# A two-layer hybrid trunk: scalings, first taps and key copies moved from VectorE to ScalarE, and the two components of differential attention combined in one step

## The chip, the cores and the metric

The kernel runs on one core of a Trainium2 chip. The metric is the time of one launch on the device, in microseconds (us), as the median of several executions. Engines are named as in the profile: PE is TensorE's matrix multiply and PEld its weight load, DVE is VectorE, ACT is ScalarE, POOL is GpSimd and SP is the queue that starts most of the DMA transfers. Each engine works its own queue strictly in order and waits on semaphores where an instruction needs another engine's result.

## The reference, cut to what matters

The program is a decoder trunk of two layers for 256 tokens of width 1024. In each layer a norm and one input projection `z = h @ w_in` (2964 columns) feed four head groups of 4 heads by 64, called A, B, C and D. Their outputs go through `w_out` into the residual, and a SwiGLU block of width 2816 follows. What the change touches:

- A (sparse attention): three softmax branches, two of which (selected blocks and window) have `o = g1 * softmax(s1) @ v1 + g2 * softmax(s2) @ v2` with gates per token and head.
- B (differential attention): `a = p[0] - lam * p[1]`, where `p` is the softmax of two score components over the same keys, then `o = rmsnorm(a @ v, sub_g) * (1 - lam_init)`. The norm divides by the root of `mean(o*o) + EPS` with EPS = 1e-6.
- C (mLSTM): a causal convolution with four taps and a bias over the 256 channels of `u`, then SiLU, then projections to q and k.
- D (dilated attention) and B both turn rotated q and k to channel-major form before their scores.

## The kernel before

All matrix products over the weights are done in three passes at full fp32 accuracy: a weight block is loaded to `wraw`, ACT rounds it to `whi` (line 224), DVE takes the rest `wlo = wraw - whi` (line 225), and `product` (lines 229 to 231) multiplies hi by hi, hi by lo and lo by hi. So each block of 128 by 1024 weights costs one ACT and one DVE instruction besides the PE work.

The input projection runs over six chunks of up to 512 columns. While PE works on the chunks, and then on `w_out`, the four mixers are laid between: each is a generator, and the table `ORDER` says how many steps of which generator are written out behind which chunk (Z and A are the two parts of A; lower-case letters transpose a finished output). That is the order of writing only. The framework's planner then sets the order on each engine from its own estimate of what is ready and how urgent it is, so in the trace the instructions of a mixer and of the projection stand finely mixed. Nothing changes order on the chip: what an engine's queue has first, it does first.

The places that the steps below name:

- A, lines 471 to 517: for each of two 128-token tiles `t` and two rounds `r`, scores come to PSUM, ACT takes the exponentials with their row sums (line 492), DVE inverts the sums and multiplies in the gates (lines 495, 496), and DVE scales the four probability matrices in place (line 499), 128 or 256 columns each. PE then transposes them (line 506, `pTa`), ACT and DVE split the result (lines 509, 510) and PE applies the values (line 516). There are eight such groups of four in the run: two layers, two tiles, two rounds.
- C, lines 579 to 599: `u` is transposed on PE, copied to `uT` on ACT (line 583), convolved on DVE (first tap with bias on line 587, three more on line 589, twice per layer), passed through tanh on ACT (593), finished on DVE (594), and projected on PE (599, `qkc`).
- `qk_T`, lines 669 to 683, for B and D: after POOL's rotation (`rope`) and PE's transposes, ACT copies q (681) and DVE copies k (682).
- B, lines 689 to 738: for each tile and each `i` two score components `c` for two heads `b`. Exponentials with row sums on ACT (707), inverses on DVE (709), times minus lambda (710), the second component scaled (712) and the combination (713), then transposes, values, and the norm, whose `rstd_of` adds EPS and takes the power -0.5 on POOL (239, 243) before POOL's final product (736).

Of the kernel before, what the change touches and what calls it, by code (L numbers as in the profile page):

```python
# [10 lines left out]
F32 = mybir.dt.float32  # L11
F32R = mybir.dt.float32r
BF = mybir.dt.bfloat16
AF = mybir.ActivationFunctionType
OP = mybir.AluOpType
# [3 lines left out]
P = 128  # L19
SEQ = 256  # L20
D = 1024
NH = 4
# [6 lines left out]
EPS = 1e-6  # L29
# [69 lines left out]
def trunk(ctx, tc, xt, w_in, w_out, w_gu, w_dn, gains, gfin, cmpw, chan, rowp, ident_d, kf, kb, out):  # L99
    nc = tc.nc  # L100
    V, S, G, T = nc.vector, nc.scalar, nc.gpsimd, nc.tensor
# [40 lines left out]
    def t4():  # L142
        i = 2 * D_IN + slot[0] % NS * 1024
        slot[0] += 1
        return cur['big'][:, i:i + 1024]
# [84 lines left out]
        T.matmul(acc, xh, wl, start=False, stop=False)  # L230
        T.matmul(acc, xl, wh, start=False, stop=last)  # L231

    def rstd_of(ms, shape, name):
        e = sm.tile([P] + shape, F32, name=name + "e")
        r = sm.tile([P] + shape, F32, name=name)
        n = 1
        for s in shape:
            n *= s
        G.tensor_scalar(e, ms, EPS, None, op0=OP.add)
        nh = nhalf[:, :n]  # L240
        if len(shape) == 2:
            nh = nh.rearrange("p (a b) -> p a b", a=shape[0])
        G.tensor_tensor(out=r, in0=e, in1=nh, op=OP.pow)
        return r
# [65 lines left out]
    def heads(ap, n):  # L310
        return ap.rearrange("p (n w) -> p n w", n=n)
# [145 lines left out]
    def mixer_a2(l, z, d):  # L457
# [13 lines left out]
        for t in range(2):  # L471
# [3 lines left out]
            for r in range(2):  # L475
# [20 lines left out]
                V.tensor_tensor(out=zs, in0=zs, in1=g4[:, t, r], op=OP.mult)  # L496
                for b in range(2):
                    for m in range(2):
                        V.tensor_scalar(pm[:, b, m, 0:ns * P], pm[:, b, m, 0:ns * P], zs[:, b, m:m + 1], None,  # L499
                                        op0=OP.mult)  # L500
                for s in range(ns):
                    pt = aux("pTa")
                    for b in range(2):
# [23 lines left out]
    def mixer_c(l, z, d, o):  # L527
# [56 lines left out]
        uc = q512("uc")  # L584
        cw = d['conv']
        for b in range(2):
            V.tensor_scalar(uc[:, b], uT[:, b, 3:259], cw[:, b, 3:4], cw[:, b, 4:5], op0=OP.mult, op1=OP.add)
            for j in (2, 1, 0):
                V.scalar_tensor_tensor(out=uc[:, b], in0=uT[:, b, j:j + 256], scalar=cw[:, b, j:j + 1], in1=uc[:, b],
                                       op0=OP.mult, op1=OP.add)  # L590
# [13 lines left out]
        qT, kT = qk  # L604
# [64 lines left out]
    def qk_T(z, col, n, hd, scale, tag, eng):  # L669
        pq = aux("qT" + tag)  # L670
        pk = aux("kT" + tag)
        for t in range(2):
            rr = w512("rqk")
            rope(eng, heads(z[:, t, col:col + 512], n), n, hd, t, heads(rr, n))
            for b in range(2):
                T.transpose(pq[:, b * SEQ + t * P:b * SEQ + (t + 1) * P], rr[:, b * P:(b + 1) * P], ident)
                T.transpose(pk[:, b * SEQ + t * P:b * SEQ + (t + 1) * P], rr[:, 256 + b * P:256 + (b + 1) * P], ident)
            yield
        qT = q512("qT" + tag)
        kT = q512("kT" + tag)  # L680
        S.activation(qT, heads(pq, 2), AF.Copy, scale=scale)
        V.tensor_copy(kT.rearrange("p b t -> p (b t)"), pk)
        return qT, kT


    def mixer_b(l, z, d, o):
        qT, kT = yield from qk_T(z, COL['bq'], 16, 16, 32.0 ** -0.5, "b", G)
        yield
        for t in range(2):
            n = P * (t + 1)  # L690
            am = heads(t4(), 4)
            for i in range(2):
                zb = sm.tile([P, 2, 2], F32, name="zb")
                nmb = sm.tile([P, 2, 2], F32, name="nmb")
                pmb = t4().rearrange("p (c b k) -> p c b k", c=2, b=2)

                scs = [heads(aux("sb")[:, 0:2 * n], 2) for _ in range(2)]
                for b in range(2):
                    for c, sc in enumerate(scs):
                        q = slice(32 * (2 * i + c), 32 * (2 * i + c) + 32)  # L700
                        T.matmul(sc[:, b], qT[q, b, t * P:(t + 1) * P], kT[q, b, 0:n], start=b == 0, stop=False)  # L701
                for sc in scs:
                    T.matmul(sc[:, :, t * P:(t + 1) * P], kbc('ident'), heads(kbc('causal'), 2), start=False, stop=True)
                for c, sc in enumerate(scs):
                    V.tensor_reduce(out=nmb[:, c], in_=sc, op=OP.max, axis=AX.X, negate=True)
                    for b in range(2):
                        S.activation(pmb[:, c, b, 0:n], sc[:, b], AF.Exp, bias=nmb[:, c, b:b + 1],
                                     accum_out=zb[:, c, b:b + 1])
                V.reciprocal(out=zb, in_=zb)
                V.tensor_scalar(zb[:, 1], zb[:, 1], d['nlam'], None, op0=OP.mult)  # L710
                for b in range(2):
                    V.tensor_scalar(pmb[:, 1, b, 0:n], pmb[:, 1, b, 0:n], zb[:, 1, b:b + 1], None, op0=OP.mult)
                    V.scalar_tensor_tensor(out=am[:, 2 * b + i, 0:n], in0=pmb[:, 0, b, 0:n], scalar=zb[:, 0, b:b + 1],
                                           in1=pmb[:, 1, b, 0:n], op0=OP.mult, op1=OP.add)
                yield
            aT = t4().rearrange("p (s h k) -> p s h k", s=2, h=NH)
            for s in range(t + 1):
# [14 lines left out]
            V.tensor_tensor(out=ob, in0=p4, in1=d['subg'][:, None, :].to_broadcast([P, NH, HD]), op=OP.mult)  # L732
            ms = sm.tile([P, NH], F32, name="bms")
            V.tensor_reduce(out=ms, in_=sq, op=OP.add, axis=AX.X)
            rr = rstd_of(ms, [NH], "brs")
            G.tensor_tensor(out=heads(o[:, t], 4), in0=ob, in1=rr[:, :, None].to_broadcast([P, NH, HD]),
                            op=OP.mult)
            yield
# [442 lines left out]
```

## Time and profile before

| | |
|---|---|
| median of 3 runs | 696.52 us (694.51 to 696.61) |
| the profiled execution's own time | 698.92 us |
| its span, first to last instruction | 697.1 us |
| PE busy | 673.1 us, 97% of the span |
| DVE busy | 473.8 us, 68% |
| ACT busy | 350.9 us, 50% |
| POOL busy | 111.3 us, 16% |
| mean granted clock of TensorE | 0.992 |

The busy share is an average over stages with different limits. A wait row names the engine that waited, the line and tile of the waiting instruction, and what ended the wait last, with the total time, the number of times and the longest. "issue" stands for time for which the profile shows no releaser. A timeline row gives start, duration, engine, line, operation, output and inputs, shape and count; several equal instructions in a row are merged, and the duration is then that of the whole run of them.

### The profile page before, as it was taken

How to read it: one execution, taken by the hardware profiler on the slowest of the kernel's cores; microseconds unless marked ns; L12 is line 12 of the kernel's file. 1: busy time of each engine (PE TensorE's matmuls, PEld its weight loads, DVE VectorE, ACT ScalarE, POOL GpSimd, SP SyncE). 2: the span in 40 equal slices, each digit the busy share in tenths (PEclk: the TensorE clock that was granted, in tenths of full speed). 3: DMA queues.
4: the chain of work that ended last, by engine and by line, in shares of the span. 5: the costliest groups of instructions: out<-in, count | busy, mean ns of one | idle time of the engine just before them, and what ended most of it. 6: DMA issues, size and time to landing. Idle time of an engine off the chain costs nothing.

```text
span 697.1 us, 11878 instructions
## 1 busy us (share of the span) xinstructions
PE 673.1 (97%) x4701; PEld 607.8 (87%) x4701; DVE 473.8 (68%) x730; ACT 350.9 (50%) x585; POOL 111.3 (16%) x118
## 2 busy tenths in 40 slices
PE   8989899999999999999999999999999999999996
PEld 5766677899999999999987667789999999998885
DVE  6698689758766766644577688995776575755443
ACT  7555556546444444433366455574635454444333
POOL 0151354100201110000012353621000000000002
PEclk9999999999999999999999899999999999999998
DMA  8863323235576656666656423322566556666641
GB/s 274 305 198 102 100 65 118 62 92 182 152 209 183 179 162 206 180 187 183 187 175 207 145 71 91 91 62 61 150 207 187 157 179 188 184 208 198 190 121 61
DMA packets 31879, 109.11 MB, mean 157 GB/s; under 512 B 3920, under 2 KB 4688, under 8 KB 31824
## 3 DMA queue, kind: packets, MB, share of 16 engines
q1 hardware_dynamic: 31392, 107.82, 51.5%
q8 instruction: 37, 0.61, 0.4%
q10 hardware_dynamic: 432, 0.54, 0.2%
q14 instruction: 18, 0.15, 0.1%
HBM read 107.30 MB, written 1.05 MB: 155 GB/s over the span
## 4 chain that ended last, share of the span: by engine, by line
PE 85%; DVE 9%; issue 2%; ACT 2%; DMA 1%; POOL 0%; SPq 0%; POOLq 0%; ACTq 0%; DVEq 0%
PE f L229 12%; PE f L230 12%; PE f L231 12%; PE dn L230 5%; PE dn L229 5%; PE dn L231 5%; PE zp L230 4%; PE zp L231 4%; PE zp L229 4%; DVE wlo L225 2%; PE op L230 2%; PE op L229 2%; PE op L231 2%; PE sb L701 1%; DVE zbig L499 1%
## 5 line engine op out<-in xcount | busy, mean ns | idle before, releaser
L225 DVE TENSOR_TENSOR wlo<-wraw,whi 128x1024 fp32r<-128x1024 f32 (+2 forms) x201 | 245.4, 1223 | 153.1 <-ACT whi L224 152.8
L224 ACT ACTIVATE whi<-wraw 128x1024 fp32r<-128x1024 f32 (+2 forms) x201 | 210.5, 1048 | 245.3 <-PE f L230 110.3
L229 PE MATMUL f<-hT,whi 128*128 128x256 f32 x704 | 199.8, 284 | 0.0
L230 PE MATMUL f<-lT,whi 128*128 128x256 f32 x704 | 199.3, 283 | 0.0
L231 PE MATMUL f<-hT,wlo 128*128 128x256 f32 x704 | 199.2, 283 | 0.0
L230 PEld LDWEIGHTS f<-lT,whi 128*128 128x128 f32 x704 | 135.0, 192 | 0.1
L229 PEld LDWEIGHTS f<-hT,whi 128*128 128x128 f32 x704 | 135.0, 192 | 0.1
L231 PEld LDWEIGHTS f<-hT,wlo 128*128 128x128 f32 x704 | 135.0, 192 | 0.0
L229 PE MATMUL zp<-whi,hT 128*128 128x512 f32 (+1 forms) x192 | 76.5, 401 | 1.0 <-ACT whi L224 1.0
L230 PE MATMUL zp<-wlo,hT 128*128 128x512 f32 (+1 forms) x192 | 76.3, 398 | 0.6 <-DVE wlo L225 0.5
L231 PE MATMUL zp<-whi,lT 128*128 128x512 f32 (+1 forms) x192 | 75.1, 392 | 0.0
L230 PE MATMUL dn<-gT,whi 128*128 128x256 f32 x176 | 49.5, 281 | 0.0
L229 PE MATMUL dn<-gT,whi 128*128 128x256 f32 x176 | 49.5, 281 | 0.0
L231 PE MATMUL dn<-gT,wlo 128*128 128x256 f32 x176 | 49.5, 281 | 0.0
L229 PEld LDWEIGHTS zp<-whi,hT 128*128 128x128 f32 x192 | 36.9, 192 | 7.4 <-ACT whi L224 1.8
L230 PEld LDWEIGHTS zp<-wlo,hT 128*128 128x128 f32 x192 | 36.7, 191 | 7.4 <-DVE wlo L225 2.2
L231 PEld LDWEIGHTS zp<-whi,lT 128*128 128x128 f32 x192 | 36.6, 191 | 5.7
L230 PE MATMUL op<-oT,whi 128*128 128x256 f32 x128 | 37.1, 290 | 0.0
L231 PE MATMUL op<-oT,wlo 128*128 128x256 f32 x128 | 36.7, 287 | 0.0
L229 PE MATMUL op<-oT,whi 128*128 128x256 f32 x128 | 36.5, 289 | 0.0
L230 PEld LDWEIGHTS dn<-gT,whi 128*128 128x128 f32 x176 | 33.1, 188 | 0.0
L229 PEld LDWEIGHTS dn<-gT,whi 128*128 128x128 f32 x176 | 33.1, 188 | 0.0
(283 smaller groups left out, 1067.8 us busy)
## 6 DMA issues: line engine op xcount, KB each, us to landing
wraw<-in_w_gu_dram SPq DMA_DIRECT2D x88, 512.0 KB, 4.2
wraw<-in_w_dn_dram SPq DMA_DIRECT2D x44, 512.0 KB, 4.1
wraw<-in_w_in_dram SPq DMA_DIRECT2D x39, 512.0 KB, 4.3
wraw<-in_w_out_dram SPq DMA_DIRECT2D x16, 512.0 KB, 3.7
wraw<-in_w_in_dram SPq DMA_DIRECT2D x8, 404.0 KB, 3.1
wraw<-in_cmpw_dram SPq DMA_DIRECT2D x4, 512.0 KB, 6.0
xr<-in_xt_dram SPq DMA_DIRECT2D x4, 256.0 KB, 6.2
chan<-in_chan_dram SPq DMA_DIRECT2D x2, 261.0 KB, 5.1
```

The lines of the kernel that those rows point to most:

```text
L224: S.activation(hi[:, c], raw[:, c], AF.Copy)
L225: V.tensor_tensor(out=lo[:, c], in0=raw[:, c], in1=hi[:, c].bitcast(F32), op=OP.subtract)
L229: T.matmul(acc, xh, wh, start=first, stop=False)
L230: T.matmul(acc, xh, wl, start=False, stop=False)
L231: T.matmul(acc, xl, wh, start=False, stop=last)
L499: V.tensor_scalar(pm[:, b, m, 0:ns * P], pm[:, b, m, 0:ns * P], zs[:, b, m:m + 1], None, op0=OP.mult)
L701: T.matmul(sc[:, b], qT[q, b, t * P:(t + 1) * P], kT[q, b, 0:n], start=b == 0, stop=False)
```

## The change

Four edits. In A, line 499's scaling becomes an ACT copy with a scale per token. In C, line 587's first tap becomes an ACT instruction with scale and bias per channel. In `qk_T`, the copy of k becomes an ACT copy like that of q. In B, the first component is no longer divided by its row sum z0: the second is multiplied by `nlam * z0 / z1` and added to the first as it stands, in one DVE instruction in place of two. The row of B's output is then too large by the factor z0, and since a norm follows, the same factor is taken out by it, if the norm's epsilon is multiplied by z0 squared: `zq = EPS * z0 * z0` is one small DVE instruction per tile, and `rstd_of` adds it as a tensor in place of the constant.

```diff
-    def rstd_of(ms, shape, name):
+    def rstd_of(ms, shape, name, eps=None):
...
-        G.tensor_scalar(e, ms, EPS, None, op0=OP.add)
+        if eps is None:
+            G.tensor_scalar(e, ms, EPS, None, op0=OP.add)
+        else:
+            G.tensor_tensor(out=e, in0=ms, in1=eps, op=OP.add)
...
-                        V.tensor_scalar(pm[:, b, m, 0:ns * P], pm[:, b, m, 0:ns * P], zs[:, b, m:m + 1], None,
-                                        op0=OP.mult)
+                        S.activation(pm[:, b, m, 0:ns * P], pm[:, b, m, 0:ns * P], AF.Copy, scale=zs[:, b, m:m + 1])
...
-            V.tensor_scalar(uc[:, b], uT[:, b, 3:259], cw[:, b, 3:4], cw[:, b, 4:5], op0=OP.mult, op1=OP.add)
+            S.activation(uc[:, b], uT[:, b, 3:259], AF.Identity, bias=cw[:, b, 4:5], scale=cw[:, b, 3:4])
...
-        V.tensor_copy(kT.rearrange("p b t -> p (b t)"), pk)
+        S.activation(kT, heads(pk, 2), AF.Copy)
...
+            z0 = sm.tile([P, 2, 2], F32, name="zb0")
             for i in range(2):
-                zb = sm.tile([P, 2, 2], F32, name="zb")
+                z1 = sm.tile([P, 2], F32, name="zb1")
...
                         S.activation(pmb[:, c, b, 0:n], sc[:, b], AF.Exp, bias=nmb[:, c, b:b + 1],
-                                     accum_out=zb[:, c, b:b + 1])
-                V.reciprocal(out=zb, in_=zb)
-                V.tensor_scalar(zb[:, 1], zb[:, 1], d['nlam'], None, op0=OP.mult)
+                                     accum_out=z1[:, b:b + 1] if c else z0[:, b, i:i + 1])
+                V.reciprocal(out=z1, in_=z1)
+                V.scalar_tensor_tensor(out=z1, in0=z1, scalar=d['nlam'], in1=z0[:, :, i], op0=OP.mult, op1=OP.mult)
                 for b in range(2):
-                    V.tensor_scalar(pmb[:, 1, b, 0:n], pmb[:, 1, b, 0:n], zb[:, 1, b:b + 1], None, op0=OP.mult)
-                    V.scalar_tensor_tensor(out=am[:, 2 * b + i, 0:n], in0=pmb[:, 0, b, 0:n], scalar=zb[:, 0, b:b + 1],
-                                           in1=pmb[:, 1, b, 0:n], op0=OP.mult, op1=OP.add)
+                    V.scalar_tensor_tensor(out=am[:, 2 * b + i, 0:n], in0=pmb[:, 1, b, 0:n], scalar=z1[:, b:b + 1],
+                                           in1=pmb[:, 0, b, 0:n], op0=OP.mult, op1=OP.add)
...
-            rr = rstd_of(ms, [NH], "brs")
+            zq = sm.tile([P, NH], F32, name="zq")
+            z0f = z0.rearrange("p b i -> p (b i)")
+            V.scalar_tensor_tensor(out=zq, in0=z0f, scalar=EPS, in1=z0f, op0=OP.mult, op1=OP.mult)
+            rr = rstd_of(ms, [NH], "brs", zq)
```

## Rows read from the trace of the kernel before

**Rows 1.** Busy time of each engine in stretches of the run. Columns: the stretch, its length, then PE, PEld, DVE, ACT and POOL busy (with instruction counts), the granted clock, the DMA share and GB/s. The mixers of layer 0 lie in the first two stretches, those of layer 1 in the last two.

```profile
52.00:122.00 70.00, 63.63 (x367) 49.76 (x368) 57.48 (x111) 39.62 (x101) 25.55 (x27) 1.00 0.33 97
122.00:157.00 35.00, 35.00 (x265) 31.46 (x265) 23.16 (x49) 16.49 (x39) 3.75 (x6) 1.00 0.26 77
...
400.00:452.00 52.00, 48.40 (x268) 37.24 (x267) 44.80 (x86) 29.28 (x74) 26.68 (x24) 1.00 0.27 79
452.00:484.00 32.00, 31.66 (x232) 26.87 (x232) 23.94 (x56) 18.79 (x55) 5.53 (x8) 1.00 0.26 79
```

**Rows 2.** Who waited for whom, PE's matrix multiplies and weight loads: total us, times, longest.

```profile
PE pTa L506 <- DVE zbig L499: 3.9, 7, 1.1
PE qkc L599 <- issue: 2.9, 2, 2.1
PE sC L626 <- DVE zbig L630: 0.8, 2, 0.6
PE aT L720 <- DVE zbig L713: 0.3, 1, 0.3
...
PEld zp L229 <- ACT whi L224: 1.8, 2, 1.4
```

**Rows 3.** Groups of equal instructions on DVE that the change removes: busy us, mean ns of one, idle time before them.

```profile
L499 DVE TENSOR_SCALAR zbig<-zbig,zsa 128x256 f32<-128x256 f32 x16 | 9.2, 624 | 0.1
...
L499 DVE TENSOR_SCALAR zbig<-zbig,zsa 128x128 f32<-128x128 f32 x16 | 6.8, 488 | 0.1
...
L712 DVE TENSOR_SCALAR zbig<-zbig,zb 128x256 f32<-128x256 f32 x8 | 2.5, 360 | 0.0
...
L587 DVE TENSOR_SCALAR uc<-uT,chan 128x256 f32<-128x256 f32 x4 | 2.3, 609 | 0.0
...
L712 DVE TENSOR_SCALAR zbig<-zbig,zb 128x128 f32<-128x128 f32 x8 | 2.0, 282 | 0.1
...
L682 DVE COPY kTb<-kTb 128x512 f32<-128x512 f32 x2 | 1.4, 688 | 0.0
```

**Rows 4.** Timeline rows, in order of time: six of the eight groups of four scalings of line 499 on DVE, the weight split that follows the first, and POOL's rotation that runs beside the first.

```profile
66.47 1.27 POOL L297 TENSOR_TENSOR rqk<-zbig,kft 128x512 f32<-128x512 f32 x1 [14.41 <-issue]
66.64 2.75 DVE L499 TENSOR_SCALAR zbig<-zbig,zsa 128x128 f32<-128x128 f32 x4
69.31 2.31 DVE L225 TENSOR_TENSOR wlo<-wraw,whi 128x1024 fp32r<-128x1024 f32 x1
...
86.58 0.88 DVE L499 TENSOR_SCALAR zbig<-zbig,zsa 128x128 f32<-128x128 f32 x4
...
417.63 2.33 DVE L499 TENSOR_SCALAR zbig<-zbig,zsa 128x128 f32<-128x128 f32 x4
...
429.84 0.87 DVE L499 TENSOR_SCALAR zbig<-zbig,zsa 128x128 f32<-128x128 f32 x4
...
436.12 3.68 DVE L499 TENSOR_SCALAR zbig<-zbig,zsa 128x256 f32<-128x256 f32 x4
...
446.56 2.43 DVE L499 TENSOR_SCALAR zbig<-zbig,zsa 128x256 f32<-128x256 f32 x4
```

**Rows 5.** What such work takes on ACT: two groups of equal instructions (a copy with a scale per partition, and an exponential with a bias per partition; columns as in rows 3), and a timeline row of two scaled copies one behind the other.

```profile
L257 ACT ACTIVATE hT<-xr,gain 128x256 fp32r<-128x256 f32 x32 | 14.4, 496 | 8.1 <-DVE xr L936 5.7 <-DMA gain<-in_gains_dram 1.4 <-DMA xr<-in_xt_dram 1.0
L492 ACT ACTIVATE zbig<-sa,nma 128x128 f32<-128x128 f32 x16 | 5.7, 360 | 2.8 <-DVE nma L490 2.8
...
158.31 0.89 ACT L257 ACTIVATE hT<-xr,gain 128x256 fp32r<-128x256 f32 x2
```

**Rows 6.** Busy time (columns as in rows 1) in four short stretches: from the end of the last product before line 506's transposes to the next product (first group of A, layer 0); around the group at 436.12; and the two pauses of PE before line 599.

```profile
66.89:69.81 2.92, 1.31 (x8) 0.84 (x9) 2.92 (x5) 1.44 (x2) 2.84 (x4) 1.00 0.51 144
77.31:79.19 1.88, 0.00 (x0) 0.03 (x1) 1.88 (x4) 1.40 (x2) 0.00 (x0) 1.00 0.00 0
411.29:412.15 0.86, 0.00 (x1) 0.03 (x1) 0.86 (x2) 0.00 (x0) 0.86 (x2) 1.00 0.89 143
437.62:440.50 2.88, 1.62 (x13) 1.17 (x12) 2.88 (x6) 0.39 (x2) 1.69 (x2) 1.00 0.00 0
```

**Rows 7.** Timeline rows of ACT at the first and the last group of A: the weight conversion that its queue holds close behind the time at which the scale factors are ready.

```profile
67.28 1.05 ACT L224 ACTIVATE whi<-wraw 128x1024 fp32r<-128x1024 f32 x1
...
446.90 1.06 ACT L224 ACTIVATE whi<-wraw 128x1024 fp32r<-128x1024 f32 x1 [0.93 <-PE zp L231]
```

**Rows 8.** Timeline rows of the convolution in C: the first taps on DVE in layers 0 and 1, and on ACT the copy to `uT` in layer 0 and layer 1 and the weight conversion beside the taps of layer 1.

```profile
70.37 0.59 ACT L583 ACTIVATE uT<-uTp 128x512 f32<-128x512 f32 x1
72.15 1.53 DVE L587 TENSOR_SCALAR uc<-uT,chan 128x256 f32<-128x256 f32 x2
...
403.82 0.60 ACT L583 ACTIVATE uT<-uTp 128x512 f32<-128x512 f32 x1 [0.36 <-PE uTp L582]
406.10 0.74 DVE L587 TENSOR_SCALAR uc<-uT,chan 128x256 f32<-128x256 f32 x2
406.34 1.07 ACT L224 ACTIVATE whi<-wraw 128x1024 fp32r<-128x1024 f32 x1 [1.93 <-PE zp L231]
```

**Rows 9.** Groups of equal instructions on POOL in the norm of B: the addition of EPS, and the power (columns as in rows 3).

```profile
L243 POOL TENSOR_TENSOR brs<-brse,nhalf 128x4 f32<-128x4 f32 x4 | 4.1, 1036 | 0.3
...
L239 POOL TENSOR_SCALAR brse<-bms 128x4 f32<-128x4 f32 x4 | 0.9, 228 | 36.6 <-DVE bms L734 36.6
```

**Rows 10.** Busy time and granted clock (columns as in rows 1) in the stretch of layer 1 where the clock falls, ahead of the changed steps.

```profile
388.00:400.00 12.00, 10.43 (x40) 7.84 (x39) 7.26 (x14) 5.29 (x9) 1.99 (x3) 0.72 0.44 127
```

## The prediction, as put on record

> **What bounds the kernel now.** I read the busy time by stage first, then who waits for whom, then the timeline at the waits that name a changed line. The page gives PE 97% of the span, but that is a mean: the reader should see in [rows 1] that PE is never idle from 122 to 157 us and for 0.34 us of 32 at the end of layer 1's mixers, while it loses 6.4 us of 70 in the first mixer stretch of layer 0 and 3.6 of 52 in that of layer 1. So there are about 10 us to be had, all in these two stretches, and whatever the change does outside them is hidden by PE. In both DVE is busy 82 to 86% and ACT 56%: DVE is the crowded neighbour, and work is moved from it to ACT.
>
> The waits say who holds PE there [rows 2]: the transposes of A wait 3.9 us for line 499's scalings on DVE, the projections of C wait 2.9 us with no releaser shown (the convolution's chain ends just before), C's score products 0.8 us for line 630. B's transposes wait 0.3 us.
>
> The timeline shows why line 499 is slow [rows 4]: four scalings of 128 columns take 0.87 to 0.88 us in two groups, but 2.33 and 2.75 in two others; four of 256 take 2.43 and 3.68. In the slow groups POOL's rotation runs beside them: the first began at 66.47, ended at 67.74, and only then DVE got on. In all, 32 scalings take 16.0 us [rows 3].
>
> **The change, part by part.**
>
> *A's scaling.* DVE loses 16.0 us. ACT gains 16 instructions of 128 columns and 16 of 256. The trace has the 256 form almost exactly, a scaled copy from SBUF of 496 ns, two in 0.89, so a step of 0.40 [rows 5]; four take 3 x 0.40 + 0.49 = 1.69 us. For 128 columns the nearest is the exponential at 360 ns [rows 5]; with a step shorter by the same 0.14, four take 3 x 0.26 + 0.36 = 1.14. ACT's bill is about 4 x 1.14 + 4 x 1.69 = 11.3 us of an engine that is idle 44% there. What it does for PE, group by group:
>
> - 66.64: factors ready at 66.62, ACT could finish by 67.8 in place of 69.39 on DVE. PE's pause there is 2.92 - 1.31 = 1.61 us [rows 6]. I take 1.5 back.
> - 436.12: DVE ends at 439.80, ACT by about 438. The pause is 2.88 - 1.62 = 1.26 [rows 6], and ACT has only 0.39 us of other work in it. I take 1.2.
> - 417.63: PE waits not for the scaling but for line 630, queued behind it on DVE; 0.6 of its 0.8 us [rows 2].
> - 446.56: ends at 448.99, ACT could end at 448.25; PE was held 0.35 of the 3.9 us. I take 0.35.
> - 86.58, 429.84 and the two groups not shown (16.0 less the six shown leaves 3.1 us for both, against 3.4 on ACT): ACT is slower than an undisturbed DVE by 0.27 (1.14 against 0.87) or 0.15 a group. Together 0.75 lost.
>
> Net -2.9. Bounds: at best all waits on lines 499 and 630 go, -4.7; at worst the scalings come out behind weight conversions on ACT, +2.2 (worked out as a rival).
>
> A rule of the Trainium skill speaks against the move: "ScalarE: Activation LUTs", Rules for kernel authors, sends multiplications to VectorE, and its section on what a table load costs prices an activation at 186 ns plus 0.833 ns a column plus 93 for each per-partition operand, with 93 of overlap. By that four of 128 columns would take 1.27 us, and each first tap with two such operands 0.59; the sum would be about 0.5 us poorer. The trace agrees only where POOL is quiet; in four groups DVE took 2.33 to 3.68.
>
> *C's first tap.* DVE loses 4 x 0.61 = 2.4 us [rows 3]. In layer 0 `uT` is ready at 70.96 and ACT then has a gap, DVE's two taps end at 73.68 [rows 8]. On ACT they end near 71.9, so line 589's taps can start where line 587's did, at 72.15, and the chain ends up to 1.5 earlier. PE's pause behind it is 1.88 [rows 6]: I take -1.4. In layer 1 `uT` is there at 404.42, ACT idles 1.93 us until 406.34, DVE's taps end at 406.84 after 0.74 us [rows 8]; pause 0.86 [rows 6]: I take -0.6. Together -2.0. Bounds: -2.7 (both pauses gone) to +0.8 (second rival). The form with two per-partition operands is not in the trace; between 0.36 and 0.61 us by the rows above, and at either end it fits into the gaps.
>
> *Copy of k.* Four copies of 0.69 us leave DVE [rows 3]; on ACT a PSUM tile of this size takes 0.59 to 0.60 [rows 8], but behind the copy of q. ACT serial against two engines side by side: 0, between -0.2 and +0.6.
>
> *B.* DVE loses 16 scalings, 4.5 us [rows 3], the two-element factor step stays, and four tiny ones are added. But PE is full in B's stretches [rows 1]; what it waits for B is 0.3 [rows 2]: -0.3. Added is `zq` between the row sums and POOL's addition, which turns from a constant to a tensor: 0.23 us now, at most the 1.04 of the power beside it [rows 9]. Behind it queue only POOL's power and final product. PE's `w_out` products cover it; uncovered at the last tile it would be 0.8 + 0.2. Bounds -0.6 to +1.0.
>
> *What is late next.* No transfer is moved, and SP's loads go out when DVE has split a block, so they can only come sooner. The added wait is ACT's on the factors of DVE's line 496: behind it in ACT's queue stand conversions [rows 7], and PE waits for these already, 1.8 us in two times [rows 2]. I charge +0.7.
>
> Sum: -2.9 - 2.0 + 0 - 0.3 + 0.7 = -4.5. The profiled execution took 698.92 us, span 697.1 and 1.8 around it; it becomes 694.4. It stood 2.4 above the median of the runs, so I predict 696.52 - 4.5 = 692.0.
>
> **The rivals.**
>
> *The stall is inherited.* POOL's rotation doesn't go away; the next DVE instruction runs into it. For: the weight split at 69.31 took 2.31 us beside POOL [rows 4]. Then the four slow groups give nothing, the quick ones still lose 0.75, line 630 loses its 0.6 of gain, B and the give-back cancel roughly, and the convolution, whose remaining taps stand beside POOL too, keeps about 1.75. Result about -1.0, 695.5. Against: PE does not wait for that split now as it does for line 499.
> "SBUF — State Buffer", Who interferes with whom, in the Trainium skill states this rule: a VectorE instruction with two SBUF inputs, or in a two-port mode, locks against GpSimd and the second to issue blocks fully, while ScalarE never waits. The rows at 66.47 to 69.31 agree; the split has two SBUF inputs, so the rule supports the move and this rival alike.
>
> *ACT's queue becomes the bound* (slower). If the planner puts the scalings behind the conversions, each waits 1.05 us [rows 7] and then takes ACT's longer time. The quick groups lose 1.05 + 0.27 each, 2.6; 66.64 ends at 68.33 + 1.14 = 69.47, 0.1 later; 446.56 at 447.96 + 1.69, 0.66 later; 436.12, with no conversion in its way, still gains 1.2; 417.63 nothing: +2.2. In layer 1 the taps would follow the conversion at 406.34 and come 1.4 later, layer 0 would still gain 0.6: +0.8. Together +3.0, 699.5. It decides from about half the groups on. For: ACT works in order and its scale factors come late. Against: the planner goes by urgency, and PE needs the transposes sooner than a block with idle time ahead of it.
>
> *The clock.* Between 388 and 400 us the granted clock means 0.72 [rows 10], so stretches at the lower of the two levels, 1.2 GHz, after PE had 1.57 us of gaps: 12 x 0.28 = 3.4 us lost. In layer 0 no such fall shows. No changed line stands there, but a new plan may close that pause: -4.5 - 3.4, 688.6.
>
> **How the numbers follow.** Forecast 0.52, its own range 690.0 to 694.6; stall inherited 0.24; ACT's queue 0.14; clock too 0.10. 0.3% is 2.1 us, about what a measurement of this kernel tells from no change: faster is below 694.4, slower above 698.6. Faster: nearly all of the forecast, the clock case and a little of the second, 0.62; same 0.25; slower 0.13. The range 687.5 to 698.5 leaves out most of ACT's queue and the far end of the clock case.
>
> **What would show it.** Right: no wait of `pTa` on a scaling above 0.5 us, the pause before `qkc` in layer 0 below 0.7 us, DVE busy about 24 us less in all, ACT some 15 more, PE idle in 52 to 122 us about 3 less. Inherited: splits or line 630 beside POOL grow to over 2 us and PE waits there. ACT's queue: `pTa` waits on ACT behind line 224. Wrong altogether: PE's idle time in both stretches as before, or a new fall of the clock.

## The result, and the profile after

The changed kernel takes 703.91 us (median of 20 runs, 696.38 to 707.64), the kernel before 697.62 in the same session (20 runs, 694.24 to 702.31): 1.0067 times as long, 95% interval 1.0040 to 1.0095. Of the twenty, the three longest (707.13 to 707.64) count as slow runs, which the ratio and its interval leave out, here and below, while the medians keep them; without them the median is 702.60. So it is slower by some 5 us where 692.0 was forecast, and outside the range.

The profiled execution shows nothing of this. It took 698.45 us, span 696.7, granted clock 0.991, while the kernel before had 698.92, 697.1 and 0.992. It is the third quickest of its twenty, and the list of runs shows why the others differ: each run's time goes with its mean granted clock. The two at 0.993 took 696.4 and 696.5 us, the five at 0.984 took 701.2 to 702.6, the eight from 0.974 to 0.978 took 704.0 to 707.6. Over all runs the mean clock is 0.982, that of the kernel before 0.992 (29 runs on one chip). So two numbers stand beside each median below: the mean clock of the runs, and the time at a clock of 0.990, read off a straight line through the runs of one kernel (for the changed kernel it falls by 5.9 us per 0.01 of clock). At that clock the changed kernel takes 698.6 us and the kernel before 699.1 to 699.7 (six sets of runs). By these lines the change saves some 0.5 to 1.1 us of work, and loses some 6 us to the clock.

Busy time of the page, after:

```profile
PE 671.9 (96%) x4701; PEld 608.2 (87%) x4701; DVE 453.2 (65%) x678; ACT 365.2 (52%) x625; POOL 108.4 (16%) x118
```

DVE is 20.6 us less busy, where about 24 was forecast, and ACT 14.3 more, where 15 was: the work moved as the diff says, and DVE lost some of the relief again to instructions beside POOL (rows below). The stretches of [rows 1] after the change:

```profile
52.00:122.00 70.00, 63.23 (x348) 49.55 (x348) 47.78 (x89) 45.81 (x117) 25.48 (x26) 0.94 0.33 97
122.00:157.00 35.00, 34.95 (x263) 31.00 (x262) 20.35 (x42) 16.67 (x43) 3.65 (x6) 0.96 0.21 61
...
400.00:452.00 52.00, 49.08 (x274) 38.31 (x272) 37.21 (x68) 37.46 (x96) 24.92 (x24) 1.00 0.29 83
452.00:484.00 32.00, 31.14 (x226) 26.47 (x224) 22.53 (x50) 18.22 (x52) 4.74 (x8) 1.00 0.29 83
```

PE idled 6.37 + 0 + 3.60 + 0.34 = 10.31 us in these before, 6.77 + 0.05 + 2.92 + 0.86 = 10.60 now. DVE is 9.7 us less busy in the first stretch, and PE gained nothing there. The waits say where the pauses went (total, times, longest):

```profile
PE qkc L601 <- issue: 2.9, 1, 2.9
PE oa L518 <- ACT pTa L511: 2.2, 2, 1.6
...
PE qTd L678 <- DVE oc L523: 1.2, 1, 1.2
...
PE sb L705 <- DVE oT L815: 0.9, 1, 0.9
PE pTa L508 <- ACT zbig L502: 0.8, 2, 0.5
...
PE kTd L679 <- ACT zbig L711: 0.7, 1, 0.7
```

The 3.9 us for which `pTa` waited on the scaling [rows 2] are 0.8. New are 2.2 us of A's products on ACT, 0.9 and 0.7 in B and D; and the two waits for the convolution, 2.1 and 0.8 us, became one of 2.9. How that came about in layer 0 (timeline of DVE and ACT; start, duration):

```profile
66.58 1.28 ACT L502 ACTIVATE zbig<-zbig,zsa 128x128 f32<-128x128 f32 x4 [0.36 <-DVE zsa L499]
...
70.23 1.09 ACT L589 ACTIVATE uc<-uT,chan 128x256 f32<-128x256 f32 x2
70.38 2.36 DVE L225 TENSOR_TENSOR wlo<-wraw,whi 128x1024 fp32r<-128x1024 f32 x1 [0.74 <-ACT whi L224]
...
72.65 4.46 DVE L591 SCALAR_TENSOR_TENSOR uc<-uT,chan,uc 128x256 f32<-128x256 f32 x6
...
77.04 1.90 DVE L225 TENSOR_TENSOR wlo<-wraw,whi 128x808 fp32r<-128x808 f32 x2
78.86 0.68 DVE L596 SCALAR_TENSOR_TENSOR uc<-th,uc 128x512 f32<-128x512 f32 x1
```

A's scalings are done at 67.86 in place of 69.39, and ACT's first taps at 71.32. But then a weight split runs into POOL's rotation and takes 2.36 us, the other taps begin at 72.65, and the planner puts two splits ahead of line 596 where one stood before. The chain ends at 79.54, PE arrives earlier, and its pause is 2.88 us. In layer 1 (ACT, around the pause of 1.60 us that `oa` has at 439.48):

```profile
437.15 0.90 ACT L502 ACTIVATE zbig<-zbig,zsa 128x256 f32<-128x256 f32 x2
440.13 0.42 ACT L661 ACTIVATE hsq<-hh 128x256 f32<-128x256 f32 x1 [2.08 <-DVE hh L659]
440.45 0.58 ACT L511 ACTIVATE pTa<-pTa 128x512 fp32r<-128x512 f32 x1
```

The scalings were done at 438.05, but in ACT's queue C's square of line 661 stands ahead of A's eviction, and waits 2.08 us for DVE, whose line is held up beside POOL (DVE and POOL):

```profile
435.91 1.92 POOL L306 TENSOR_TENSOR rqk<-rqk,rope 128x512 f32<-128x512 f32 x1
436.61 1.50 DVE L525 TENSOR_TENSOR oT<-oc,oT 128x256 fp32r<-128x256 f32 x1
437.91 1.36 POOL L300 TENSOR_TENSOR rqk<-zbig,kft 128x512 f32<-128x512 f32 x1
438.04 1.25 DVE L656 TENSOR_TENSOR den<-den,emt 128x4 f32<-128x4 f32 x1
```

Line 656 takes 0.27 us at the median of its four, line 525 0.42. Last the clock, in steps of 2 us behind the pauses at 76.76 and 115.41:

```profile
78.00:80.00 2.00, 0.36 (x2) 0.36 (x3) 2.00 (x4) 0.55 (x1) 0.00 (x0) 1.00 0.46 80
80.00:82.00 2.00, 2.00 (x7) 1.58 (x6) 0.45 (x1) 0.60 (x1) 0.00 (x0) 0.53 0.96 379
...
116.00:118.00 2.00, 0.70 (x5) 0.46 (x5) 1.89 (x5) 1.95 (x10) 0.18 (x1) 0.91 0.89 258
118.00:120.00 2.00, 2.00 (x12) 1.45 (x13) 1.42 (x6) 0.70 (x2) 0.00 (x0) 0.50 0.01 4
...
122.00:124.00 2.00, 2.00 (x11) 1.70 (x11) 1.17 (x5) 0.80 (x6) 0.00 (x0) 0.50 0.00 0
```

TensorE runs at the lower level, 1.2 GHz, for 3 to 4 us and again for some 7, each time after PE had idled. The profile of before had one fall, in [rows 10].

### The profile page after: what moved, and what is told of

The parts are those of the page before. It is cut to its first block, busy times and chain, and to the rows that moved or that the text cites. A ratio compares the mean times of both kernels' runs of the same rounds, so it can differ in the third digit from the quotient of the medians.

```text
span 696.7 us, 11849 instructions
## 1 busy us (share of the span) xinstructions
PE 671.9 (96%) x4701; PEld 608.2 (87%) x4701; DVE 453.2 (65%) x678; ACT 365.2 (52%) x625; POOL 108.4 (16%) x118
## 4 chain that ended last, share of the span: by engine, by line
PE 86%; DVE 7%; ACT 3%; issue 2%; DMA 1%; POOL 0%; SPq 0%; POOLq 0%; ACTq 0%; DVEq 0%
PE f L229 12%; PE f L230 12%; PE f L231 12%; PE dn L230 5%; PE dn L229 5%; PE dn L231 5%; PE zp L230 4%; PE zp L231 4%; PE zp L229 4%; DVE wlo L225 3%; PE op L229 2%; PE op L230 2%; PE op L231 2%; PE sb L705 2%; ACT whi L224 1%
## 5 line engine op out<-in xcount | busy, mean ns | idle before, releaser
L229 PEld LDWEIGHTS dn<-gT,whi 128*128 128x128 f32 x176 | 33.8, 192 | 0.0
L230 PEld LDWEIGHTS dn<-gT,whi 128*128 128x128 f32 x176 | 33.8, 192 | 0.0
```

The costliest lines, as they stand in the source:

```text
L229: T.matmul(acc, xh, wh, start=first, stop=False)
```

## The experiments

**Each part alone.** Four kernels: the kernel before with line 499's edit (e1), with line 587's (e2), with B's (e3), and the changed kernel with the first tap back on VectorE (e4). Each edit is its line of the diff above; the copy of k was not run by itself. In these four expectations theory 3 is B's norm; in the later ones it is a clock that falls for another reason than pauses.

> The kernel before with A's scaling alone on ScalarE. Theory 1 (the clock: the changed kernel's work is a little shorter, and it is slower because longer pauses of TensorE before the projections of C and in the first steps of B let the granted clock fall more often): the waits of the transposes on the scalings go, 3.9 us before, the chain of C is untouched, so 1 to 3 us faster than before at an equal mean clock, and the median 0 to 3 us faster. Theory 2 (ScalarE's queue: the scalings hold up the conversions and each other): 2 us or more slower than before, also among runs of equal clock. Theory 3 (B's longer norm chain): no difference to theory 1 here.

> The kernel before with C's first tap alone on ScalarE. Theory 1: if the pause before C's projections grows as in the changed kernel (2.05 us before, 2.88 after), the clock falls in most runs and the median is 2 to 5 us slower, with single runs as fast as before. Theory 2: the tap is small on ScalarE, within 1 us of before. Theory 3: as before.

> The kernel before with B's one-step combination and the row sum in the norm's epsilon alone. Theory 1: within 1 us of before at an equal clock; the median moves only if the pauses around 115 to 118 us move the clock. Theory 2: as before. Theory 3: 1 us or more slower at an equal clock.

> The changed kernel with C's first tap back on VectorE. Theory 1: the pause before C's projections is 2 us or less, the clock falls less often than in the changed kernel, median 3 us or more below the changed kernel's (that was 0.67% above before). Theory 2: still about 0.5% above before, since A's scalings are still on ScalarE. Theory 3: the same.

| kernel | median us (runs) | ratio to before, 95% | mean clock | us at 0.990 |
|---|---|---|---|---|
| before, same chip | 696.71 (29) | | 0.992 | 699.4 |
| e1, A alone | 704.49 (12) | 1.0093 (1.0056 to 1.0129) | 0.980 | 699.2 (its runs end at 0.989) |
| e2, C alone | 700.65 (12) | 1.0049 (1.0018 to 1.0079) | 0.987 | 699.4 |
| e3, B alone | 700.82 (12) | 1.0046 (1.0021 to 1.0071) | 0.987 | 699.8 |
| e4, all but C | 706.41 (6) | 1.0107 (1.0069 to 1.0146) | 0.980 | all below 0.990 |

Each part alone is slower, and at equal clock e1 to e3 are within 0.4 us of the kernel before: what they lose is clock, most of it with A's scaling. That speaks against theory 2 in e1 (2 us or more slower at equal clock) and against theory 3 in e3. Two expectations failed. e1's median was to be up to 3 us below the kernel before and is 8 above, and its gain at equal clock, to be 1 to 3 us, is 0.2. e4 was to lie 3 us or more below the changed kernel, with a pause before `qkc` of 2 us or less; it lies 2.5 above, and the pause is longer than before although the first tap is back on VectorE. So it is in e1 (first row; the second is e4's):

```profile
PE qkc L598 <- issue: 3.3, 1, 3.3
PE qkc L601 <- issue: 3.4, 1, 3.4
```

It was 2.1 us before: of what A's scaling saved in the waits of `pTa`, 1.2 to 1.3 us came back in this wait. In e2 the wait for the convolution fell from 2.9 us (2.1 and 0.8) to 0.6, and others lost as much together: D's transposes 1.1 us, C's scores 0.6 and A's transposes 0.5.

```profile
PE pTa L506 <- DVE zbig L499: 4.4, 8, 1.1
...
PE qTd L676 <- ACT zbig L707: 2.3, 1, 2.3
...
PE sC L626 <- DVE zbig L630: 1.4, 2, 1.2
...
PE qkc L599 <- issue: 0.6, 1, 0.6
```

(e2's time is as theory 1 had it, but that was for a pause that grows.) e3 is slower although PE idles 6.26 + 0 + 3.65 + 0.40 = 10.31 us in the stretches of [rows 1], as long as before. In its profile the clock falls in the last of them, where PE had idled 0.40 us in the 12 us ahead; PE ran B's score products (`sb`, 32 rows) and those of `w_out` there:

```profile
52.00:122.00 70.00, 63.74 (x368) 49.83 (x369) 57.54 (x112) 39.64 (x100) 25.50 (x26) 1.00 0.33 97
122.00:157.00 35.00, 35.00 (x274) 31.56 (x272) 22.20 (x43) 17.31 (x39) 3.66 (x6) 1.00 0.28 79
...
400.00:452.00 52.00, 48.35 (x264) 37.41 (x264) 42.93 (x85) 28.37 (x75) 27.14 (x24) 0.97 0.30 85
...
448.00:460.00 12.00, 11.60 (x72) 9.01 (x72) 9.05 (x23) 8.44 (x26) 2.65 (x3) 1.00 0.19 49
460.00:472.00 12.00, 12.00 (x52) 9.56 (x51) 7.20 (x16) 5.47 (x19) 1.83 (x3) 0.57 0.26 84
...
452.00:484.00 32.00, 31.60 (x189) 25.77 (x187) 20.31 (x46) 18.00 (x50) 4.53 (x8) 0.84 0.17 50
```

**Pauses filled, and a pause added.** Products of the identity with itself (128 columns, some 0.25 us of PE each by the profile) are put into PE's finished queue ahead of the instruction that waits, into a bank that the next real product clears. No other instruction moves.

```diff
+    for at, bank, count in sites:              # after the planner is done
+        for k in range(count):
+            nc.tensor.matmul(bank[:, 0:128], ident, ident, start=True, stop=True)
+            # ... and moved ahead of `at` in PE's queue
```

> The changed kernel with products without use put into three of PE's pauses, nothing else moved: ten products of 128 columns into the pause before the qkc products of layer 0 (2.88 us in the profile of after), four before the qTd transposes of layer 0 (1.20 and 0.69 us), five before the csT transposes of layer 1 (1.61 us); each overwrites a PSUM bank that the next real product clears. Theory 1 (the clock: the change saves about 1.8 us of work, but its pauses on PE bring TensorE's granted clock down to 1.2 GHz in more places): with the pauses filled the mean granted clock rises from 0.982 to 0.988 or more, no fall in 76-90 us, and the time falls from 704 to 694-699, ratio to before 0.995 to 1.001. Theory 2 (ScalarE's queue, or another wait, is what costs): PE only waits with other instructions in its queue, the time stays at 702-706, ratio 1.005 to 1.010. Theory 3 (the clock falls, but for a reason other than the pauses, such as the load of the other engines): the mean clock stays near 0.982 and the time at 702-706.

> The kernel before with the same three places filled (seven, four and five products), nothing else moved: the control. Theory 1: the kernel before loses 5.3 us of its time to the low clock by its runs (time times one minus the mean clock), part of it behind these pauses, so the mean clock rises from 0.992 to 0.993-0.996 and the time falls to 694-697, ratio 0.995 to 1.000, and it stays slower than the filled changed kernel or equal to it (692.4 against 690.6 at full clock). Theories 2 and 3: no change within 0.3%, 696-699.

> The changed kernel with only the first of the three places filled (ten products before the qkc products of layer 0). Theory 1: the fall at 80-84 us goes, the one at 116-126 us stays; the mean clock rises to 0.984-0.988 and the time is between the changed kernel and the one with three places filled, 698-702. Theories 2 and 3: 702-706 at a mean clock of 0.982.

e8 puts multiplications of constants by one into DVE's finished queue, ahead of the last tap.

> The kernel before with a longer pause of PE and no other change: five multiplications by one (128 columns each, of constants, about 0.2-0.3 us each) are put into VectorE's queue ahead of the last tap of the convolution of layer 0, so the qkc products of layer 0 come 1.0-1.4 us later than in the kernel before, and the pause there is 3.0-3.5 us instead of 2.05. Theory 1: the time grows by more than the pause, by 3-6 us, to 700-704, ratio 1.004 to 1.009, with a fall of the clock behind the pause and a mean clock of 0.983-0.989. Theories 2 and 3: it grows by the pause alone, by 1.0-1.4 us at most, ratio up to 1.002, mean clock unchanged at 0.992.

| kernel | median us (runs) | ratio to before, 95% | mean clock | us at 0.990 |
|---|---|---|---|---|
| before, same chip | 697.25 (35) | | 0.992 | 699.3 |
| e5, changed, three places filled | 698.78 (12) | 1.0004 (0.9972 to 1.0036) | 0.990 | 698.6 |
| e6, before, three places filled | 697.52 (12) | 1.0004 (0.9980 to 1.0028) | 0.993 | 699.4 |
| e7, changed, `qkc` alone filled | 703.65 (12) | 1.0071 (1.0034 to 1.0108) | 0.984 | 698.4 |
| e8, before, pause added | 700.58 (12) | 1.0045 (1.0018 to 1.0073) | 0.989 | 700.0 |

(One run of e7, of 3332.86 us, is left out of its last two columns.) e5 fits theory 1 and neither rival: 19 products, which only add work to PE, bring some 5 us back. e6 hardly moves, and misses theory 1's 694 to 697; it came out as theories 2 and 3 had it. e7 fails: the largest pause is filled, no fall is left at 80 us in its profile, and nothing is won. In e8 the chain grew by less than expected, about 0.7 us (the added rows take 0.61 and 0.21), which is the 0.7 by which it stands above the kernel before at equal clock; the other 2.6 us of its 3.3 are clock. The time is as theory 1 had it, the mechanism is not: the pause was to be 3.0 to 3.5 us long, and in the one profile of e8 it is shorter than before, and the falls are not behind it. One stands behind the pause that PE always had at 67 us,

```profile
66.00:70.00 4.00, 2.49 (x12) 1.43 (x10) 3.93 (x7) 2.73 (x7) 2.69 (x4) 1.00 0.70 202
70.00:74.00 4.00, 3.90 (x13) 3.26 (x14) 4.00 (x5) 1.08 (x2) 4.00 (x3) 0.57 0.15 23
```

and stretched PE's work ahead of `qkc`; the pause there was 1.07 us. So e8 does not show what a longer pause does.

**Which pauses.** The same filling in other places of the changed kernel, and A's scaling divided (`V.tensor_scalar(...) if ns == 2 else S.activation(...)`, e11).

> The changed kernel with products without use only in the stretch 104-118 us (layer 0, A's last groups, the mixer B's scores and D's transposes): two before the pTa transposes, two before the oa products, five before the qTd and three before the kTd transposes, nothing else moved; PE idles 4.0 us between 104 and 126 us in the profile of after and 1.2 us in that of before. Theory 1a (the low clock of the changed kernel comes above all from this stretch, since every profile of a kernel with A's scaling on ScalarE shows a fall behind it, and filling the pause before the qkc products alone, which left the median at 703.65, could not help it): no fall of the granted clock in 112-140 us, mean clock 0.986-0.990, time 698-701, ratio 1.001 to 1.005. Theory 1b (all pauses of the program count alike): 3 us of idle time fewer of some 15, mean clock 0.983-0.985, time 702-703. Theory 2 (other engines, not the clock): 703-705.

> The changed kernel with all the larger pauses filled, nothing else moved: the places of e9, twelve products before the qkc products of layer 0, and in layer 1 six before csT, six before the oa products behind the pause of 1.60 us at 439 us and three before the sb products behind 0.87 us at 458 us. Theory 1 (the clock): the mean clock is 0.992 or more, the falls left are few, and the time is 693-697, which is below the kernel before (697.3): ratio 0.994 to 0.999. If the clock falls also where PE hardly idles, the mean clock stays at 0.990 as with three places filled, and the time at 697-699, ratio 1.000 to 1.003.

> The changed kernel with A's scaling on ScalarE only for the first half of the queries (pieces of 128 columns) and back on VectorE for the second half (256 columns, four in 1.71 us on ScalarE): the order of the engines is the same up to some 104 us of layer 0. Theory 1a: the 256-column pieces make ScalarE the late engine in 104-118 us; with them back on VectorE PE idles 1-2 us there instead of 4.0, no fall behind it, mean clock 0.986-0.991, time 698-701, the work at full clock 691-692. Theory 1b or another place: mean clock 0.980-0.984 as before, time 702-706.

> The control to e10: the kernel before with its own larger pauses filled, nothing else moved: four products before the pTa transposes of layer 0 behind the pause of 1.09 us at 67 us, eight before the qkc products (2.05 us), five before the qTd transposes (1.23 us), and in layer 1 six before csT (1.56 us), three before qkc (0.86 us), four before the pTa transposes (1.04 us). Theory 1 (the change saves 1.8 us of work and loses more to the clock): with both kernels' pauses filled the clock is alike, 0.994-0.996, so the filled kernel before is at 695-697.5, above the filled changed kernel by 0-2 us; its own gain over the kernel before is smaller than e10's gain over the changed kernel (some 6 us), 1-3 us, since it has fewer falls to lose: ratio 0.995 to 1.000. Theory 4 (the products without use speed a kernel up for a reason of their own, whatever the change does): the same 6 us fall from the kernel before, to 691-693.

> The changed kernel with only the places of layer 1 filled (six products before csT, six before the oa products at 439 us, three before the sb products at 458 us). Filling the pause before the qkc products alone left 703.65 us and the stretch 104-118 us alone 704.85, so by elimination, if each place counts by itself (theory 1c), what e10 won (from 704 to 697.5) lies in these: 697-700 at a mean clock of 0.989-0.993. If a fall needs all pauses around to be filled (theory 1d: layers 0 and 1 each have their falls, and each is cured by its own), layer 1 alone gives about half: 700-702 at 0.985-0.988. Without effect (703-705) both fall.

> The changed kernel with only the pause before the csT transposes of layer 1 filled (six products; 1.61 us). The kernel before has the same pause (1.56 us). Theory 1c with csT as the place: 698-700, mean clock 0.988-0.991. If the pauses that the change made in layer 1 (1.60 us at 439 us, 0.87 us at 458 us) are what counts: 702-704, mean clock 0.982-0.985.

> The changed kernel with only two places of layer 1 filled, the pauses that the change brought there: six products before the oa products at 439 us (1.60 us) and three before the sb products at 458 us (0.87 us). e13 (these and csT) gave back 4.8 us and e14 (csT alone) 1.7. If the places add up, these two give 3.1: 700-702, mean clock 0.985-0.988. If csT and these must be filled together, 702.5-704.5 at 0.981-0.984. If these two alone carry layer 1's part, 698.5-700 at 0.989 or more.

| kernel | median us (12 runs each) | ratio to before, 95% | mean clock | us at 0.990 |
|---|---|---|---|---|
| e9, changed, 104 to 118 us filled | 704.85 | 1.0079 (1.0046 to 1.0111) | 0.981 | all below 0.990 |
| e10, changed, all places filled | 697.47 | 0.9963 (0.9938 to 0.9987) | 0.994 | 698.3 |
| e11, changed, A's second half on VectorE | 700.64 | 1.0004 (0.9976 to 1.0033) | 0.986 | 697.4 |
| e12, before, all places filled | 696.83 | 0.9962 (0.9931 to 0.9992) | 0.994 | 699.6 |
| e13, changed, layer 1 filled | 699.07 | 0.9989 (0.9958 to 1.0019) | 0.990 | 698.5 |
| e14, changed, `csT` alone filled | 702.25 | 1.0027 (0.9996 to 1.0057) | 0.984 | 698.6 |
| e18, changed, 439 and 458 us alone filled | 701.50 | 1.0035 (1.0001 to 1.0069) | 0.986 | 698.5 |

(The kernel before stood at 699.31 us beside e9 to e11, 698.74 beside e12 to e14, where a run of 817.02 us is left out of the line against the clock, and 697.78 beside e18.) e10 shows the loss undone, a little above the time expected: it stands at 0.9963 of the kernel before, the changed kernel at 1.0067. It has 27 products more than e9, beside it on the same chip, and takes 7.4 us less. Its profile, taken of a run at a clock of 0.999, has no fall in the mixers of either layer. The two whole stretches, 40 to 146 and 372 to 490 us, first of after, then of e10:

```profile
40.00:146.00 106.00, 96.81 (x562) 76.61 (x561) 74.70 (x153) 64.64 (x163) 38.16 (x41) 0.95 0.30 91
372.00:490.00 118.00, 112.25 (x684) 91.04 (x683) 84.68 (x169) 75.28 (x178) 40.93 (x43) 1.00 0.37 107
```

```profile
40.00:146.00 106.00, 102.22 (x640) 83.23 (x640) 75.86 (x155) 66.37 (x165) 38.48 (x41) 1.00 0.32 96
372.00:490.00 118.00, 115.72 (x729) 95.13 (x728) 84.50 (x168) 74.53 (x178) 40.92 (x43) 1.00 0.36 104
```

The control e12 takes theory 4 away: the same means gives the kernel before 1.9 us, not 6. Theory 1a fell with e9: PE was kept busy in 104 to 126 us (idle 22.00 - 21.37 = 0.63; in after 22.00 - 18.69 = 3.31, not the 4.0 of the expectation), and the clock still fell right behind it, in a stretch where PE did not idle at all. The first row is after's, the others are e9's:

```profile
104.00:126.00 22.00, 18.69 (x115) 15.06 (x113) 13.21 (x32) 13.65 (x39) 9.08 (x11) 0.84 0.23 72
...
104.00:126.00 22.00, 21.37 (x149) 17.69 (x147) 14.32 (x33) 14.92 (x45) 8.76 (x11) 1.00 0.23 70
126.00:134.00 8.00, 8.00 (x34) 6.35 (x34) 5.15 (x15) 4.34 (x16) 1.83 (x3) 0.57 0.00 0
```

Which places carry the loss stays open. By the ratios, `csT` alone takes the changed kernel from 1.0067 to 1.0027, the two pauses that the change made at 439 and 458 us to 1.0035, the three together (e13) to 0.9989, all places to 0.9963; `qkc` alone and the middle stretch change nothing. e13, e14 and e18 came out as expected if the places of layer 1 add up. But the intervals of e14 and e18 overlap that of the changed kernel, the pause before `csT` is no work of the change (1.57 us before, 1.61 after), and e5 gives back nearly as much as e13 (to 1.0004) with `csT` as its only place in layer 1. So these runs do not tell how much each place carries.

e11 came out in the time and clock that theory 1a gave it, but not by its mechanism: PE idled 2.09 us in 104 to 118 us of its profile, and the clock was 0.57 in the 8 us behind, where no fall was to be. It is the quickest kernel at equal clock (697.4), and loses it to the clock again.

**Filled against filled.** Since e10 and e12 came out alike on two chips, both ran once more on one, with e11's kernel filled as well.

> e10 once more, beside e12's kernel on the same chip: the filled changed kernel against the filled kernel before, with the clock nearly out of it. If the change saves work that lasts (0.7 to 2 us by the lines of time against clock), it is below the filled kernel before by 0.5-2 us at the same mean clock; if its work only moved PE's pauses, the two are equal within 0.5 us. 695-698, ratio to before 0.994 to 0.999.

> e12 once more, the partner of the run above: 695.5-698, ratio 0.995 to 0.999.

> The kernel of e11 (A's scaling on ScalarE for the first half of the queries only) with its own larger pauses filled: eleven products before the qkc products of layer 0, two before the pTa transposes at 111 us, six before the qTd transposes, and in layer 1 six before csT and four before the pTa transposes at 442 us. e11 has the least work of all by time times clock (689.9). Theory 1: with the clock at 0.993 or more it is at 693-696, the fastest of all, ratio 0.991 to 0.997. If its low product comes from the many falls in it (a slower PE hides other waits) and not from less work, it is equal to the other two filled kernels: 696-698, ratio 0.995 to 0.999.

| kernel | median us (12 runs each) | ratio to before, 95% | mean clock | us at 0.990 |
|---|---|---|---|---|
| e15, changed, all places filled | 696.99 | 0.9992 (0.9960 to 1.0024) | 0.993 | 698.9 |
| e16, before, all places filled | 697.83 | 0.9998 (0.9965 to 1.0031) | 0.992 | 699.4 |
| e17, e11's kernel filled | 698.98 | 1.0001 (0.9968 to 1.0033) | 0.989 | 698.4 |

The kernel before had 698.82 us beside them. The filled kernels cannot be told from it here, so e10's and e12's gains of 0.4% did not repeat, none of these versions is shown to beat the kernel before, and e17 failed both its theories. What did repeat is that the changed kernel, once filled, no longer lies 0.67% above the kernel before. e15 is the program of e10, and its profiled run, at 0.993, has the fall that e10's lacks, behind 0.62 us of PE's idle time:

```profile
104.00:126.00 22.00, 21.38 (x147) 17.33 (x146) 14.19 (x34) 16.01 (x51) 9.02 (x12) 1.00 0.18 51
126.00:134.00 8.00, 8.00 (x43) 7.40 (x41) 4.81 (x12) 3.85 (x12) 0.43 (x1) 0.57 0.10 17
```

The profiles of e5 and e6 have one there too (126 to 134 and 128 to 136 us), and in all of them PE works on B's and D's score products at the time. In the runs of e10, e12, e15 and e16 at 0.997 or more, where hardly a fall is left, the filled changed kernel took 694.4 us (mean of 8) and the filled kernel before 695.0 (mean of 9): 0.6 us of work, where the sum had 4.5. Of e11's advantage at equal clock half is gone in e17 (1.2 us against 2.2), as it would be if a slower PE hides other waits; that is not shown.

## Why the prediction was wrong

**What the sum left out.** It counted TensorE's clock as it was. Of its rivals one let a fall of the clock vanish with the pause before it; a new fall stood only in the last sentence, without a price or a chance. That is the step that failed most: by the runs, 0.010 of mean clock, some 6 us, the whole of the loss. The profile of before already showed a fall behind 1.57 us of gaps [rows 10], and the price of one, 3.4 us, was worked out; the step not taken was to ask it of a new plan at all. Both signs that the prediction named for being wrong altogether came: PE's idle time as before, and new falls of the clock. The prediction also held that what the change does outside the two mixer stretches is hidden by PE; from 122 to 157 us PE is as busy as before (34.95 of 35), and the granted clock there is 0.96 in place of 1.00.

**A's scaling, -2.9.** Right in the waits that it named: those of `pTa` fell from 3.9 to 0.8 us, and the stretch at 66.89 [rows 6] had 1.61 us of PE's idle time and has

```profile
66.89:69.81 2.92, 2.88 (x17) 2.19 (x17) 0.69 (x1) 2.92 (x8) 2.84 (x4) 1.00 0.50 142
```

0.04; the longest `pTa` wait on a scaling is 0.51 us. Four of 256 columns took 1.71 us (1.69 in the text), four of 128 took 1.28 (1.14); by the text's own figures its four quick groups lose 0.84, not 0.75. The estimate from "ScalarE: Activation LUTs" of the Trainium skill, its section on what a table load costs, was 1.27 for four of 128; the trace agrees. What failed is that PE would keep these gains: in layer 0 they came back before `qkc` (e1 and e4), at 436 us the scalings came out early and the eviction behind them waited in ACT's queue, so that PE's pause of 1.26 us became one of 1.60, and after 115 us PE idles 1.20 + 0.69 us in D's transposes where 1.23 had been.

**C's first tap, -2.0.** The tap itself was priced well (0.596 us, bounds 0.36 to 0.61), and in e2 the pause of layer 0 shrank as forecast. In layer 1 the pause of 0.86 us went, in good part by luck: the last tap ends at 409.05 in place of 409.21, and the step behind it takes 1.06 us less, although POOL's rotation runs beside it in both (the first row is before's, the second after's).

```profile
410.31 1.74 DVE L594 SCALAR_TENSOR_TENSOR uc<-th,uc 128x512 f32<-128x512 f32 x1
410.11 0.68 DVE L596 SCALAR_TENSOR_TENSOR uc<-th,uc 128x512 f32<-128x512 f32 x1
```

In layer 0 of the changed kernel it failed at "line 589's taps can start where line 587's did, at 72.15": they start at 72.65 behind a split of 2.36 us, and end behind one split more. The pause was to shrink by 1.4 us and grew by 0.8. Not all of that is the tap's: with A's scaling moved and the tap left on VectorE (e4) it is longer still, 3.4 us.

**The rivals.** *The stall is inherited* is what the timeline shows at 70.38, 436.61 and 438.04. The rule that was cited for it, "SBUF — State Buffer", Who interferes with whom, in the Trainium skill, fits these rows: all three are DVE instructions with two inputs in SBUF, beside POOL's rotation, at 1.23, 0.42 and 0.27 us elsewhere. Its price, 695.5, left the clock out too. *ACT's queue becomes the bound* had the right sign for another reason: one group of scalings stood behind a conversion (factors at 434.47, first scaling at 435.33), and no product waited for it; an eviction stood behind C's square, and that wait cost 1.6 us once.

**B, the copy of k, "late next".** B's wait for combinations is gone, line 740's product takes 0.16 us and POOL's addition 0.243 in place of 0.228: nothing, as said. The copy of k takes 0.59 to 0.61 us on ACT; no run has it alone. The +0.7 for what is late next was far too small: the gains of A and C in PE's waits, some 4 us, were given back whole elsewhere, as the idle sums 10.31 and 10.60 show. At equal clock the sum of -4.5 came to about -0.7.

**Shown and not shown.** Shown: the loss is in the granted clock (time at equal clock), and it goes when several of PE's larger pauses are filled with products while everything else stays (e5, e10, e13, e15). Not settled: which pause brings which fall, and whether it is pauses alone. The falls of e3, e9 and e15 shown above had next to no pause ahead of them, and the runs of one kernel spread from 0.974 to 0.993 with the same instructions. Two rivals stand untested. The work that PE does in B's stretches, where those falls lie, may count beside the pauses. And the kernel before may be a plan that happens to fall seldom, so that any new plan loses: three unlike edits each lost clock, B's with hardly a pause changed. Whether it is the added work or the absence of the pause that keeps the clock up, these experiments do not separate.

## What to carry to other kernels

Where PE is over 90% busy and the clock falls anywhere in the profile, give a fall of the clock behind PE's new or moved pauses a price and a chance, and do not go by the work that is taken from other engines alone: here moving 20 us off DVE saved about 1 us at most and cost some 6 in clock. Before explaining a difference by waits, set each run's time against its mean granted clock; it takes no extra run, and it told here that the profiled execution of the changed kernel, at 0.991 where its runs mean 0.982, was no witness of the loss. And when work moves to an engine with a strict queue, look for what its next instruction waits for, not only for what the moved one costs.

## What was not expected of the hardware

- Three edits that each leave the time at equal clock as it was (699.2, 699.4, 699.8 against 699.4 us) each made the kernel 0.5 to 0.9% slower, through the clock.
- Products without any use made a kernel faster: 39 of them, some 10 us of PE's time, took the changed kernel from 1.0067 of the kernel before to 0.9963 and 0.9992.
- The clock can fall where PE had idled only 0.63 us in the 22 us ahead (126 to 134 us in e9), and the same program can have this fall in one profiled run (e15) and not in another (e10).
